# Output products of mixing and attention: seven products after Strassen in place of eight blocks, low parts of the right sums by accumulating DMA

## The chip, the cores and the metric

The kernel runs on one core of one Trainium2 chip. The metric is the time of one execution in microseconds of the device. The kernel before has a median of 1040.52 us over 3 runs (1040.29 to 1040.53).

## The reference

One decoder layer on 512 tokens of width 1024, in float32, each step followed by a layer norm of `alpha*h + sublayer(h)`:

1. a SwiGLU FFN at half weight (inner width 2816);
2. token mixing: one input projection, whose columns go to a gated linear recurrence in four heads of 128 (q, forget gate, input, output gate) and to causal pooling in four groups; the 512 columns of the heads and the 512 of the pooling are put side by side and mapped by `w_mix_out` (1024 x 1024);
3. cross-attention of four heads of 256 into 256 memory tokens, mapped by `wo` (1024 x 1024);
4. a second SwiGLU FFN at half weight.

```python
merged = jnp.concatenate([o, p], axis=-1); return merged @ w_out        # mixing
o = jnp.einsum('bhsm,bmhd->bshd', p, v).reshape(b_, s_, D_MODEL); return o @ wo   # attention
```

## The kernel before, in words

**Float32 by three products.** TensorE multiplies in a reduced float32 (`F32R`). So every operand x is split into a high part, a cast of x on ScalarE, and a low part, x minus the high part on VectorE (`split`, lines 66 to 68); a product is high x high + high x low + low x high, three matmuls into one PSUM bank (`mm3`, line 55). A weight block is 128 x 1024 (512 KB): `wblock` (lines 71 to 82) loads it from HBM on SP's queue into a raw tile and splits it.

**Tiles.** `b8` is a ring of 13 tiles of 8 KB per partition, `raw` and `q` are rings of 7 tiles of 4 KB (raw blocks; high or low parts), PSUM has six banks `mm` and two `tr`. The program order is a priority: the framework orders each engine's queue ahead of time by what it takes to be ready, so a later operation can be drawn forward while an earlier one waits. The queues themselves run in order.

**The two FFNs** already use Strassen's method with seven products for both of their matrices. For the output matrix (`strassen_gemm`, lines 325 to 454) the right-hand sums t1 to t4 of the weights are formed in HBM: `Sums` (lines 266 to 313) lists copies of a block into scratch and accumulating DMAs into it, all on POOL's queue. `one_behind` (lines 317 to 323) issues the next listed action behind a weight block, after a tiny POOL operation that reads this block; `pace` says behind which share of the blocks. The second FFN's 48 actions begin behind the query weights of mixing at a pace of 2/3 (lines 677 to 679); what is left is issued by `step` (line 304) inside the second FFN.

**Mixing.** Projections for the forget gates and queries (lines 669 to 682); pooled groups, gates and the levels of the scan (lines 703 to 837); states, head outputs and their norm (lines 842 to 890), with the keys of the memory, `mem_key(0)` to `(2)`, between them. The transposed head outputs are gated and split into `mg[0]`, `mg[1]` (lines 893 to 905); the pooled part was split into `mg[2]`, `mg[3]` as it came (lines 743 to 749).

**The output product** `out_gemm` (lines 206 to 258) runs for mixing (line 907) and attention (line 1000). The four row tiles of 128 tokens have 8 k tiles and two halves of 512 columns: 2 x 4 x 8 x 3 = 192 matmuls of 128 x 128 by 128 x 512. The first half runs block by block over all row tiles. The second keeps its four weight blocks and runs row tile by row tile; after each come the add into h, the statistics, the layer norm (`ln_tile`, lines 167 to 182, whose power is POOL's) and the transposes with their splits (`transpose_h`, lines 184 to 203), while the next row tile is multiplied.

**Around it.** After mixing come the memory keys 3 to 7 and the memory values (lines 910 to 927), which don't need h. Attention's loop is lines 984 to 998: queries (`xq`), `scores`, `attend` (the transposes of P and their split), `values`, which splits each head's output into `oT`. Attention's output product loads the second FFN's first two weight blocks through `pre` (line 1002).

Of the kernel before, what the change touches and what calls it, by code (L numbers as in the profile page):

```python
# [16 lines left out]
P = 128  # L17
S = 512
# [16 lines left out]
def layer_kernel(ctx: ExitStack, tc: tile.TileContext, a, out):  # L35
# [170 lines left out]
    def out_gemm(wsrc, nkt, act, alpha, g, b, eps, name, final=False, order=None, stay=4, ys=None, pre=None):  # L206
        nb = nkt // 2
        order = list(range(nb)) if order is None else order
        tiles = None
        stats = [st.tile([P, 2, 6], F32, tag=f"stats{t}", name=f"stats{t}", bufs=1) for t in range(NT)]  # L210
        for hf in range(2):
            ps = [None] * NT
            head = nb - (2 if hf == 0 else stay)

            def part(t, i, w):
                if ps[t] is None:
                    ps[t] = mm_ps(f"{name}ps{hf}{t}")
                hi, lo = w
                for j in range(2):
                    ah, al = act(order[i] * 2 + j)  # L220
                    tsl = slice(t * P, (t + 1) * P)
                    wh, wl = hi[:, j * 512:(j + 1) * 512], lo[:, j * 512:(j + 1) * 512]
                    nc.tensor.matmul(ps[t], ah[:, tsl], wh, start=i == 0 and j == 0, stop=False)  # L223
                    nc.tensor.matmul(ps[t], ah[:, tsl], wl, start=False, stop=False)  # L224
                    nc.tensor.matmul(ps[t], al[:, tsl], wh, start=False, stop=i == nb - 1 and j == 1)  # L225

            for i in range(head):
                w = wblock(wsrc[hf, order[i]], f"{name}{hf}_{i}")
                for t in range(NT):
                    part(t, i, w)  # L230
            ws = [wblock(wsrc[hf, order[i]], f"{name}{hf}_{i}", stay=hf == 1 and i < head + 3) for i in range(head, nb)]
            if hf == 1:
                GB = ln_bcast(g, b)
                if pre is not None:
                    pre()
            for t in range(NT):
                for i, w in enumerate(ws):
                    part(t, head + i, w)
                sl = slice(hf * 512, hf * 512 + 512)
                nc.vector.scalar_tensor_tensor(  # L240
                    out=h[t][:, sl], in0=h[t][:, sl], scalar=float(alpha), in1=ps[t],
                    op0=ALU.mult, op1=ALU.add)
                nc.vector.bn_stats(stats[t][:, hf, :], h[t][:, sl])
                if hf == 1:
                    ln_tile(t, stats[t], GB, eps)
                    if final:
                        for q in range(2):
                            nc.sync.dma_start(out[t * P:(t + 1) * P, q * 512:(q + 1) * 512], h[t][:, q * 512:(q + 1) * 512])
                    else:
                        if t == 0:  # L250
                            tiles = [quarter(f"{name}T{q}") if ys is not None else b8([P, 2, 2, S], F32R, f"{name}T{q}")
                                     for q in range(4)]
                        transpose_h(t, tiles, ys)
        if final:
            return None
        if ys is not None:
            return tiles
        return [(tiles[k // 2][:, k % 2, 0, :], tiles[k // 2][:, k % 2, 1, :]) for k in range(KT)]

# [6 lines left out]
    class Sums:  # L266


        def __init__(self, wsrc, name, kb1, kb2):
            self.w, self.name, self.kb1, self.kb2, self.T = wsrc, name, kb1, kb2, {}  # L270
            self.copies = [(p, b) for some in (("t1", "t3", "t2"), ("t4",)) for b in range(len(kb1)) for p in some]
            self.adds = list(self.copies)

# [51 lines left out]
    def strassen_gemm(groups, S_, alpha, g, b, eps, name, final=False, pre=None, ys=None):  # L325
# [61 lines left out]
        if len(groups) == 1:  # L387
            quarter_["s1"] = [raw4([P, 4, 256], f"{name}s1")]
        else:
            s1 = b8([P, 2, 4, 256], F32, f"{name}s1")  # L390
            s1_ = [sm.tile([P, n, 256], F32, tag="s1", name=f"{name}s1_{n}", bufs=2) for n in (2, 1)]
            quarter_["s1"] = [s1[:, 0], s1[:, 1], *s1_]
# [61 lines left out]
        return [(tiles[k // 2][:, k % 2, 0, :], tiles[k // 2][:, k % 2, 1, :]) for k in range(KT)]  # L454

# [212 lines left out]
    T0 = b8([P, H * S], F32, "T0")  # L668
    pf01 = proj_T2(wf, X1, "pf")
# [7 lines left out]
    sums2 = Sums(a["w2out"], "f2", *FFN_BLOCKS)  # L677
    todo_behind += sums2.actions()
    pace[:] = 0, 2, 3
# [35 lines left out]
    mg = {q: b8([P, 2, 2, S], F32R, f"mg{q}") for q in (2, 3)}  # L715

    def mslot(k):
        return mg[k // 2][:, k % 2, 0, :], mg[k // 2][:, k % 2, 1, :]

# [23 lines left out]
    def pool_out(g):  # L743
        pm = mm_ps("pm")
        nc.tensor.matmul(pm, pw[:, g, :], pooled[g], start=True, stop=True)
        mh, ml = mslot(4 + g)
# [119 lines left out]
    for q in range(2):  # L866
        mg[q] = b8([P, 2, 2, S], F32R, f"mg{q}")
# [211 lines left out]
```

## Time and profile before

| | us |
|---|---|
| median of 3 runs | 1040.52 |
| the profiled execution, as timed | 1040.28 |
| its span, first to last instruction | 1038.5 |
| PE busy | 1024.5 (99%), 6898 matmuls |
| DVE busy | 830.7 (80%), 1360 instructions |
| ACT busy | 508.3 (49%) |
| POOL busy | 137.4 (13%) |

Engines: PE is TensorE's matmuls, PEld its weight loads, DVE VectorE, ACT ScalarE, POOL GpSimd; SP's queue only issues DMAs. PE's busy time is modelled with overlapping ends: a matmul of 512 columns is shown with 0.39 us, and the next starts long before that. So its speed is read from start to start, and its waits from the list of waits. A window row gives, for a stretch, busy time and (number of instructions) of each engine, then the granted TensorE clock (1.00 is 2.4 GHz), the DMA engines' busy share and their GB/s. Mixing's output product lies at about 490 to 538 us, attention's at 644 to 694 us, the second FFN from 694 us on.

### The profile page before, as it was taken

How to read it: one execution, taken by the hardware profiler on the slowest of the kernel's cores; microseconds unless marked ns; L12 is line 12 of the kernel's file. 1: busy time of each engine (PE TensorE's matmuls, PEld its weight loads, DVE VectorE, ACT ScalarE, POOL GpSimd, SP SyncE). 2: the span in 40 equal slices, each digit the busy share in tenths (PEclk: the TensorE clock that was granted, in tenths of full speed). 3: DMA queues.
4: the chain of work that ended last, by engine and by line, in shares of the span. 5: the costliest groups of instructions: out<-in, count | busy, mean ns of one | idle time of the engine just before them, and what ended most of it. 6: DMA issues, size and time to landing. Idle time of an engine off the chain costs nothing. (4 is left out here: it accounts for less than half of the span.)

```text
span 1038.5 us, 17839 instructions
## 1 busy us (share of the span) xinstructions
PE 1024.5 (99%) x6898; PEld 926.9 (89%) x6898; DVE 830.7 (80%) x1360; ACT 508.3 (49%) x879; POOL 137.4 (13%) x212
## 2 busy tenths in 40 slices
PE   9999999999999999999999999999999999999995
PEld 8999999998887988879888988889999999988884
DVE  7999888889989645886686356589988888889885
ACT  5566555566644422235324345236555555565731
POOL 0011111215200101002212100110000000025000
PEclk9999999999999999999999999999999999999998
DMA  9375776578966455544819741603333332359761
GB/s 359 130 243 164 220 230 201 144 232 263 285 212 241 145 155 150 148 128 131 239 60 339 207 110 61 203 23 123 90 104 124 100 102 86 119 178 241 240 236 68
DMA packets 46148, 177.36 MB, mean 171 GB/s; under 512 B 6512, under 2 KB 7792, under 8 KB 42736
## 3 DMA queue, kind: packets, MB, share of 16 engines
q1 hardware_dynamic: 40176, 130.09, 36.3%
q0 software_dynamic: 5888, 46.14, 18.0%
q8 instruction: 54, 0.88, 0.3%
q14 instruction: 30, 0.25, 0.1%
HBM read 174.11 MB, written 48.23 MB: 214 GB/s over the span
## 5 line engine op out<-in xcount | busy, mean ns | idle before, releaser
L547 PE MATMUL f2u<-xt,qf2s 128*128 128x256 f32 x480 | 60.7, 283 | 0.0
L547 PE MATMUL f1u<-xt,qf1s 128*128 128x256 f32 x480 | 60.7, 283 | 0.0
L547 PEld LDWEIGHTS f1u<-xt,qf1s 128*128 128x128 f32 x480 | 59.0, 192 | 0.0
L547 PEld LDWEIGHTS f2u<-xt,qf2s 128*128 128x128 f32 x480 | 59.0, 192 | 0.0
L174 POOL TENSOR_TENSOR rstd<-ve,mhalf 128x1 f32<-128x1 f32 x16 | 15.6, 973 | 153.9 <-DVE ve L172 153.9
L68 DVE TENSOR_TENSOR wlo_wv<-raw_wv,whi_wv 128x1024 fp32r<-128x1024 f32 x12 | 14.7, 1224 | 23.4 <-PE pq L57 8.5
L547 PE MATMUL f2w<-xoT,qf2a 128*128 128x256 f32 x240 | 32.1, 284 | 0.0
L547 PE MATMUL f1u<-xT,qf1a 128*128 128x256 f32 x240 | 32.1, 283 | 0.0
L547 PE MATMUL f2u<-xoT,qf2a 128*128 128x256 f32 x240 | 32.1, 283 | 0.0
L547 PE MATMUL f1w<-xT,qf1a 128*128 128x256 f32 x240 | 32.1, 284 | 0.0
L307 POOL TENSOR_TENSOR seen<-qf2a,mhalf 128x1 f32<-128x1 f32 x10 | 5.9, 593 | 188.2 <-ACT qf2a L67 188.2
L547 PE MATMUL f1u<-xt,qf1a 128*128 128x256 f32 x240 | 30.7, 284 | 0.0
L547 PE MATMUL f1v<-xt,qf1s 128*128 128x256 f32 x240 | 30.7, 284 | 0.0
L547 PE MATMUL f2v<-xt,qf2s 128*128 128x256 f32 x240 | 30.4, 284 | 0.0
L547 PE MATMUL f1v<-xT,qf1s 128*128 128x256 f32 x240 | 30.4, 283 | 0.0
L547 PE MATMUL f2v<-xoT,qf2s 128*128 128x256 f32 x240 | 30.4, 284 | 0.0
L547 PE MATMUL f2u<-xt,qf2a 128*128 128x256 f32 x240 | 30.4, 283 | 0.0
L547 PEld LDWEIGHTS f1w<-xT,qf1a 128*128 128x128 f32 x240 | 30.3, 192 | 0.1
L547 PEld LDWEIGHTS f2w<-xoT,qf2a 128*128 128x128 f32 x240 | 30.3, 192 | 0.0
L547 PEld LDWEIGHTS f1u<-xT,qf1a 128*128 128x128 f32 x240 | 30.2, 192 | 0.0
L547 PEld LDWEIGHTS f2u<-xoT,qf2a 128*128 128x128 f32 x240 | 30.2, 192 | 0.0
L547 PEld LDWEIGHTS f1u<-xt,qf1a 128*128 128x128 f32 x240 | 29.6, 192 | 0.1
(435 smaller groups left out, 3305.8 us busy)
## 6 DMA issues: line engine op xcount, KB each, us to landing
f1t<-in_w1out POOLq DMA_DIRECT2D x30, 512.0 KB, 8.0
f2t<-in_w2out POOLq DMA_DIRECT2D x30, 512.0 KB, 6.6
raw_f1t<-f1t SPq DMA_DIRECT2D x20, 512.0 KB, 4.4
raw_f2t<-f2t SPq DMA_DIRECT2D x20, 512.0 KB, 4.9
raw_f2g<-in_w2in SPq DMA_DIRECT2D x17, 512.0 KB, 3.7
raw_f2u<-in_w2in SPq DMA_DIRECT2D x17, 512.0 KB, 3.8
raw_f1u<-in_w1in SPq DMA_DIRECT2D x15, 512.0 KB, 5.9
raw_f1b<-in_w1out SPq DMA_DIRECT2D x15, 512.0 KB, 7.5
```

Source lines behind the costliest of these rows:

```text
L68: nc.vector.tensor_tensor(out=lo, in0=src, in1=hi.bitcast(F32), op=ALU.subtract)
L174: nc.gpsimd.tensor_tensor(out=rstd, in0=ve, in1=mhalf[:, 0:1], op=ALU.pow)
L307: ins = nc.gpsimd.tensor_tensor(out=seen, in0=q[:, 0, 0:1].bitcast(F32), in1=mhalf[:, 0:1], op=ALU.mult).ins
L547: nc.tensor.matmul(o, q[:, w, wsl], x[k][r], start=opens and k == 0 and n == 0, stop=ends and k == 3 and n == 2, skip_group_check=True)
```

## The change

Both calls of `out_gemm` become `strassen_heads`, and `out_gemm` goes. With A cut into token halves and k halves, and the weights into k halves and column halves, the seven products are a11 x b11, s1 x t1, s2 x t2, a12 x b21, s4 x b22, s3 x t3 and a22 x t4; s1 to s4 are formed on VectorE in place. They go into six PSUM banks (u, v, w, two row tiles each); u and v are added into h in between, and u is opened a second time for a22 x t4. For this, the pooled part, the head outputs and the attention outputs are kept as plain float32 (`mgp`, `mgh`, `OT`) and no longer split when they come.

The t blocks of both matrices are formed in HBM by `Sums`, as the FFNs' are: 16 actions for each matrix, listed ahead of the second FFN's 48. Their split is different (`by_dma`): ScalarE writes the high part, and then minus the high part into the low part's tile; a DMA on POOL's queue adds the raw block from HBM onto that. These blocks stay in `b8` tiles until used. t1 and t2 of mixing are split after `mem_key(0)` and before `mem_key(1)`, those of attention after the last queries; t3 and t4 inside the product. The memory keys 3 to 7 are handed to mixing's product as `fill`, ahead of its transposes.

```diff
-    def wblock(src, name, stay=False):
+    def wblock(src, name, stay=False, by_dma=False):
...
-        split(raw, hi, lo)
+        if by_dma:
+
+            nc.scalar.copy(out=hi, in_=raw)
+            nc.scalar.activation(lo, hi.bitcast(F32), AF.Copy, scale=-1.0)
+            nc.gpsimd.dma_start(lo, src, accum_op=ALU.add, max_dma_last_dim=8192)
+        else:
+            split(raw, hi, lo)
...
+    def sum_blocks(S_, name, *which):
+
+        for p in which:
+            for i in range(2):
+                assert (p, i) in S_.T and (p, i) not in S_.adds
+                S_.ready[p, i] = wblock(S_.T[p, i], f"{name}{p}{i}", True, True)
+
+    def strassen_heads(A1, A2, S_, alpha, g, b, eps, name, ys=None, fill=None, pre=None):
...
+        product(left("a11"), "b11", u, True)
+        combine("s1", "a21", "a22", ALU.subtract)
+        L = left("s1")
+        for t in range(2):
+            add(t, 0, u[t], True)
+        product(L, "t1", v, True)
+        combine("a21", "a11", "a21", ALU.subtract)
+        combine("a11", "s1", "a11", ALU.subtract)
+        L = left("a11")
+        for t in range(2):
+            add(2 + t, 1, v[t], True)
+        product(L, "t2", u)
+        L = left("a12")
+        for t in range(2):
+            add(t, 1, u[t], True, ALU.subtract)
+        product(L, "b21", w, True, True)
+        combine("a12", "a12", "a11", ALU.add)
+        L, L3 = left("a12"), left("a21")
+        for t in range(2):
+            add(t, 0, w[t], False, last=True)
+        B22 = list(right("b22"))
+        sum_blocks(S_, name, "t3", "t4")
+        L4, T3, T4 = left("a22"), list(right("t3")), list(right("t4"))
+        GB = ln_bcast(g, b)
+        for t in by_tiles(L, B22, v, True):
+            add(t, 1, v[t], False, last=True)
+            ln_tile(t, stats[t], GB, eps)
+        for t in by_tiles(L3, T3, u):
+            add(2 + t, 1, u[t], False, ALU.subtract, last=True)
+        tiles = [quarter(f"{name}T{q}") if ys is not None else b8([P, 2, 2, S], F32R, f"{name}T{q}") for q in range(4)]
+        if fill is None:
+            transpose_h(0, tiles, ys)
+        for t in by_tiles(L4, T4, u, True):
+            if fill is None and t == 0:
+                transpose_h(1, tiles, ys)
+            add(2 + t, 0, u[t], True, last=True)
+            ln_tile(2 + t, stats[2 + t], GB, eps)
+            if t == 0 and pre is not None:
+                pre()
+        if fill is not None:
+            fill()
+        for t in range(0 if fill is not None else 2, NT):
+            transpose_h(t, tiles, ys)
...
+    sums_mo = Sums(a["wmixo"], "mo", [2, 3], [0, 1])
+    sums_xo = Sums(a["wo"], "xo", [0, 1], [2, 3])
+    sums2 = Sums(a["w2out"], "f2", *FFN_BLOCKS)
+    todo_behind += sums_mo.actions() + sums_xo.actions() + sums2.actions()
+    pace[:] = 0, 1, 1
     pf01 = proj_T2(wf, X1, "pf")
...
-    sums2 = Sums(a["w2out"], "f2", *FFN_BLOCKS)
-    todo_behind += sums2.actions()
-    pace[:] = 0, 2, 3
...
     mem_key(0)
+    pace[:] = 0, 0, 1
+    sum_blocks(sums_mo, "mo", "t1")
...
+    sum_blocks(sums_mo, "mo", "t2")
     for k in range(1, 3):
         mem_key(k)
...
+    def more_keys():
+        pace[:] = 0, 4, 5
+        for k in range(3, KT):
+            mem_key(k)
+
+    pace[:] = 0, 0, 1
+    X2 = strassen_heads(mg[1], mg[0], sums_mo, ALPHA, a["ln2_g"], a["ln2_b"], LN_EPS, "mo", fill=more_keys)
...
     xq(3)
+    pace[:] = 0, 0, 1
+    sum_blocks(sums_xo, "xo", "t1", "t2")
...
+    X3 = strassen_heads(*OT, sums_xo, ALPHA, a["ln3_g"], a["ln3_b"], LN_EPS, "xo", ys=ys,
+                        pre=lambda: wx.extend(wblock(a["w2in"][u * FT], f"f2{'gu'[u]}0") for u in range(2)))
```

In the functions that are not shown, `left(p)` splits a quarter of A into a `b8` tile, `right(p)` gives the two blocks of b11, b21, b22 by `wblock` or the ready blocks of a sum, `product` runs block by block over both row tiles, `by_tiles` row tile by row tile, and `add` adds a bank into h and, at the last add of a half, takes its statistics.

## Rows read from the trace of the kernel before

**Rows 1.** The page, from its head and its first part: the span, and busy time (share of the span) and instructions of an engine.

```profile
span 1038.5 us, 17839 instructions
...
PE 1024.5 (99%) x6898; PEld 926.9 (89%) x6898; DVE 830.7 (80%) x1360; ACT 508.3 (49%) x879; POOL 137.4 (13%) x212
```

**Rows 2.** The timeline of PE in mixing's query projections, the first and the last of 96 matmuls of 512 columns: start (us), shown duration (us), engine, line, operation, out<-in, shapes, count.

```profile
361.29 0.39 PE L56 MATMUL pq<-f1T,whi_wq 128*128 128x512 f32 x1
...
382.83 0.39 PE L58 MATMUL pq<-f1T,wlo_wq 128*128 128x512 f32 x1
```

**Rows 3.** The list of waits of PE between 340 and 720 us, all of it: tile and line that waited <- engine, tile and line that released it: us in total, times, longest.

```profile
PE trh L192 <- DVE h L180: 0.5, 1, 0.5
PE po L56 <- ACT PT L67: 0.2, 1, 0.2
```

**Rows 4.** Windows of 20 us: PE, PEld, DVE, ACT, POOL busy (instructions), granted clock, DMA share, GB/s.

```profile
540.00:560.00 20.00, 20.00 (x144) 18.72 (x143) 15.49 (x26) 9.68 (x17) 4.97 (x9) 1.00 0.86 277
560.00:580.00 20.00, 20.00 (x107) 17.28 (x106) 10.44 (x11) 9.16 (x11) 4.30 (x10) 1.00 1.01 334
...
660.00:680.00 20.00, 19.50 (x90) 15.91 (x89) 13.30 (x20) 2.32 (x3) 1.00 (x2) 1.00 0.34 122
680.00:700.00 20.00, 20.00 (x122) 17.29 (x121) 17.82 (x32) 7.58 (x13) 2.96 (x3) 1.00 0.08 27
700.00:720.00 20.00, 19.97 (x166) 19.57 (x165) 17.92 (x29) 11.88 (x21) 0.00 (x0) 1.00 0.38 133
```

**Rows 5.** Windows again, with the instructions alone that touch the output product's banks: mixing's, then attention's. The first pair is PE's matmuls, then PEld and DVE.

```profile
480.00:550.00 70.00, 45.72 (x192) 35.63 (x192) 5.48 (x8) 1.00 0.50 148
...
640.00:700.00 60.00, 45.47 (x192) 35.84 (x192) 5.48 (x8) 1.00 0.30 97
```

**Rows 6.** Groups of DVE between 480 and 700 us, by line: out<-in, shapes, count | busy us, mean ns of one | idle us before them and who ended it.

```profile
L177 DVE SCALAR_TENSOR_TENSOR h<-h,mv,G 128x512 f32<-128x512 f32 x16 | 11.2, 744 | 0.0
L243 DVE BATCH_NORM_STATS2 stats<-h 128x6 f32<-128x512 f32 x16 | 11.1, 693 | 0.4
L180 DVE SCALAR_TENSOR_TENSOR h<-h,rstd,B 128x512 f32<-128x512 f32 x15 | 10.6, 746 | 0.1
...
L240 DVE SCALAR_TENSOR_TENSOR h<-h,xops 128x512 f32<-128x512 f32 x8 | 5.5, 684 | 4.3 <-PE xops L225 4.3
...
L68 DVE TENSOR_TENSOR wlo_mo<-raw_mo,whi_mo 128x1024 fp32r<-128x1024 f32 x4 | 4.9, 1219 | 1.1 <-issue 1.1
L68 DVE TENSOR_TENSOR xoT<-trh,xoT 128x512 fp32r<-128x512 f32 x6 | 4.1, 688 | 2.3 <-ACT xoT L67 2.3
...
L900 DVE SCALAR_TENSOR_TENSOR og<-ot,gn,GS 128x512 f32<-128x512 f32 x4 | 2.9, 745 | 0.0
...
L170 DVE BATCH_NORM_AGGREGATE mv<-stats 128x2 f32<-128x12 f32 x8 | 1.6, 205 | 0.1
...
L172 DVE TENSOR_SCALAR ve<-mv 128x1 f32<-128x1 f32 x8 | 1.2, 153 | 0.2
```

**Rows 7.** The timeline of ACT: two casts of 1024 columns in mixing's product, the two casts of P after the queries, the copy of a head's output.

```profile
494.89 1.99 ACT L67 CAST ws_mo<-raw_mo 128x1024 fp32r<-128x1024 f32 x2
...
630.04 1.07 ACT L67 CAST PT<-pt 128x512 fp32r<-128x512 f32 x2
...
646.47 0.59 ACT L67 CAST oT<-po 128x512 fp32r<-128x512 f32 x1 [2.16 <-PE po L58]
```

**Rows 8.** The timeline of PE around the end of the head outputs and of the attention outputs: the first output matmul drawn in, the last transposes; the first output matmul drawn in, the last of the values.

```profile
490.38 0.48 PE L223 MATMUL mops<-whi_mo,mg 128*128 128x512 f32 x1
...
492.91 0.60 PE L898 MATMUL ot<-ident,o 128*128 128x128 f32 x4
...
644.44 0.40 PE L223 MATMUL xops<-whi_xo,oT 128*128 128x512 f32 x1
...
647.18 0.39 PE L58 MATMUL po<-PT,VM 128*128 128x512 f32 x1
```

**Rows 9.** The list of waits of ACT in the second FFN, from 740 to 900 us, a line of it.

```profile
ACT qf2s L67 <- PE f2u L547: 19.6, 31, 0.8
```

**Rows 10.** The timeline of POOL: the issue of a sum in HBM, beside mixing's product.

```profile
491.74 0.85 POOL L290 DMA_DIRECT2D f2t<-f2t  x1 [0.30 <-issue]
```

**Rows 11.** DMA: a queue's packets, MB, share of 16 engines; then issues, out<-in, queue, count, KB each, median us from issue to landing.

```profile
q0 software_dynamic: 5888, 46.14, 18.0%
...
f1t<-in_w1out POOLq DMA_DIRECT2D x30, 512.0 KB, 8.0
...
raw_f2u<-in_w2in SPq DMA_DIRECT2D x17, 512.0 KB, 3.8
...
raw_f1u<-in_w1in SPq DMA_DIRECT2D x15, 512.0 KB, 5.9
...
f2t<-f2t POOLq DMA_DIRECT2D x10, 512.0 KB, 7.3
...
raw_mo<-in_wmixo SPq DMA_DIRECT2D x8, 512.0 KB, 3.8
```

**Rows 12.** Windows of the first and of the second FFN, amid their inner products; columns as in rows 4.

```profile
140.00:160.00 20.00, 20.00 (x169) 20.00 (x168) 17.27 (x33) 11.38 (x22) 3.19 (x5) 1.00 0.70 212
780.00:800.00 20.00, 20.00 (x169) 20.00 (x168) 17.27 (x33) 11.39 (x22) 0.63 (x1) 1.00 0.26 79
```

More of the change, by code (lines that the diff above doesn't have):

```diff
@@ L203, in transpose_h @@
                 nc.scalar.copy(out=ys[t // 2][:, t % 2, hf * 4:hf * 4 + 4, :], in_=ps.rearrange("p (k n) -> p k n", k=4))
[L206 to L258, printed above, removed]
@@ L272, in __init__ @@
             self.adds = list(self.copies)
+            self.ready = {}
         def copy(self, behind):
@@ L386, in strassen_gemm @@
         L = left("a11")
[L387 to L392, printed above, removed]
+        s1 = b8([P, 2, 4, 256], F32, f"{name}s1")
+        s1_ = [sm.tile([P, n, 256], F32, tag="s1", name=f"{name}s1_{n}", bufs=2) for n in (2, 1)]
+        quarter_["s1"] = [s1[:, 0], s1[:, 1], *s1_]
         product(L, "b11", u, True)
@@ L712, in layer_kernel @@
         nc.vector.tensor_tensor(out=QP[:, hd, :], in0=QP[:, hd, :], in1=T0[:, hd * S:(hd + 1) * S], op=ALU.mult)
-    mg = {q: b8([P, 2, 2, S], F32R, f"mg{q}") for q in (2, 3)}
-    def mslot(k):
-        return mg[k // 2][:, k % 2, 0, :], mg[k // 2][:, k % 2, 1, :]
+    mg = [None, b8([P, 4, S], F32, "mgp")]
     pooled = {}
@@ L745, in pool_out @@
         nc.tensor.matmul(pm, pw[:, g, :], pooled[g], start=True, stop=True)
[L746 to L749 removed]
+        nc.scalar.activation(mg[1][:, g, :], pm, AF.Copy, scale=psc[:, g:g + 1])
     pool_in(3)
@@ L864, in layer_kernel @@
         states.append(Sn)
-    for q in range(2):
-        mg[q] = b8([P, 2, 2, S], F32R, f"mg{q}")
+    mg[0] = b8([P, 4, S], F32, "mgh")
     os_ = []
@@ L898, in layer_kernel @@
             nc.tensor.transpose(pt[:, hs], o[:, hs], ident)
-        og = sm.tile([P, S], F32, tag="sg", name="og")
         nc.vector.scalar_tensor_tensor(
-            out=og.rearrange("p (h d) -> p h d", h=H), in0=pt.rearrange("p (h d) -> p h d", h=H),
+            out=mg[0][:, :, cs], in0=pt.rearrange("p (h d) -> p h d", h=H),
             scalar=gn[:, 0:1], in1=GS[:, :, cs], op0=ALU.mult, op1=ALU.mult)
-        ov = og.rearrange("p (a b n) -> p a b n", a=2, b=2)
-        for q in range(2):
-            split(ov[:, q], mg[q][:, :, 0, cs], mg[q][:, :, 1, cs])
-    X2 = out_gemm(a["wmixo"], KT, mslot, ALPHA, a["ln2_g"], a["ln2_b"], LN_EPS, "mo", order=[2, 3, 0, 1])
-    for k in range(3, KT):
-        mem_key(k)
+    def more_keys():
[4 more added lines that the diff above has]
+    X2 = strassen_heads(mg[1], mg[0], sums_mo, ALPHA, a["ln2_g"], a["ln2_b"], LN_EPS, "mo", fill=more_keys)
     VM = [b8([P, 2, D], F32R, f"VM{q}") for q in range(2)]
@@ L980, in values @@
                 mm3(po, VM[m][:, 0, csl], VM[m][:, 1, csl], PT[:, m, 0, :], PT[:, m, 1, :], m == 0, m == 1)
-            split(po, oT[:, j, 0, :], oT[:, j, 1, :])
-        OT[hd] = oT
+            nc.scalar.copy(out=OT[hd // 2][:, 2 * (hd % 2) + j, :], in_=po)
     xq(0)
@@ L999, in layer_kernel @@
     ys, wx = [], []
-    X3 = out_gemm(a["wo"], KT, lambda k: (OT[k // 2][:, k % 2, 0, :], OT[k // 2][:, k % 2, 1, :]),
-                  ALPHA, a["ln3_g"], a["ln3_b"], LN_EPS, "xo", ys=ys,
-                  pre=lambda: wx.extend(wblock(a["w2in"][u * FT], f"f2{'gu'[u]}0") for u in range(2)))
+    pace[:] = 0, 0, 1
+    X3 = strassen_heads(*OT, sums_xo, ALPHA, a["ln3_g"], a["ln3_b"], LN_EPS, "xo", ys=ys,
+                        pre=lambda: wx.extend(wblock(a["w2in"][u * FT], f"f2{'gu'[u]}0") for u in range(2)))
     todo_behind.clear()
```

54 lines of the change are left out of this document (49 added, 5 removed).

## The prediction

> **What bounds the kernel now.** I read the page first: TensorE (PE) is busy 1024.5 of 1038.5 us, and VectorE (DVE) 830.7 [rows 1]. Busy PE time is modelled, so I went to the timeline for the start times. In one projection the first and the last of 96 matmuls of 512 columns start 21.54 us apart, which is 0.227 us from start to start, and nothing stands between them [rows 2]. The list of PE's waits between 340 and 720 us has two entries, 0.7 us together [rows 3]. So here PE is the bound almost everywhere: a matmul taken away is a gain, and any new wait of PE is a loss. The windows by stage say what is close behind. Between 540 and 720 us DVE has 10 to 18 of 20 us, most of it (17.8 and 17.9) from 680 us on, where attention's output product ends and the second FFN begins; the DMA engines are at 0.86 to 1.01 between 540 and 580 us, and the granted clock is full [rows 4].
>
> **What the change removes.** Each of the two output products has 192 matmuls of 512 columns [rows 5]. Seven products of half size, each 2 row tiles x 4 k tiles x 3 matmuls = 24, are 168. That is 24 less per product, 48 in all: 48 x 0.227 = 10.9 us of PE. Nothing else of PE's work changes. With no new wait the profiled execution's own 1040.28 us would become 1029.4. It stands 0.24 us below the median of the runs shown, 1040.52; I add that at the end.
>
> **What it adds on DVE.** Prices: 1.2 us for 1024 columns, 0.69 for an add into h or a statistic, and for one layer norm 0.2 + 0.15 + 2 x 0.74 + 2 x 0.75 = 3.3 [rows 6]. From the start of product t1 to the end of t4 PE has six products, 6 x 24 x 0.227 = 32.7 us. In the same stretch DVE has 3 combinations and 5 splits of 1024 columns (9.6 us), the low parts of b21 and b22 (4 blocks, 4.8), 12 adds (8.3), 6 statistics (4.1) and two layer norms (6.7): 33.5 us. The low parts of the eight t blocks are no longer DVE's; they would have been 9.6 us more. DVE and PE are thus even in this stretch, and each hand-over that is not covered shows on PE. There are four places.
>
> (a) *The first left sum.* Before t1, the chain from the last data is: in mixing og 0.75, combination 1.2, cast on ScalarE (ACT) 1.05 [rows 7], subtraction 1.2, and some 0.1 for each of four hand-overs, 4.6 us. PE covers it with a11 x b11, 24 matmuls. In the kernel before, 8 output matmuls were already drawn in among the four transposes; then 16 x 0.227 = 3.6 us are left, and PE waits 1.0. In attention a copy (0.59) takes the place of og: 4.4 us, against 21 matmuls or 4.8 us left, since three were drawn ahead there [rows 8]. I take 1.0 + 0. Bounds: 0, if other work is drawn in; 4.6 + 4.4 = 9.0, if all of b11 has run before.
>
> (b) *t4 writes into the banks that t3 filled.* Those must first be added into h. In program order these adds stand behind both layer norms of the first two row tiles, which begin when the first half of b22 is done. From there DVE has 2 x (0.69 + 0.69 + 3.3) + 0.69 = 10.1 us; PE has half of b22 and t3, 8.2 us. In attention that is 1.9 us of waiting, and I take 2.0. In mixing the memory keys can run in the freed banks of w; I take 0.5. Bounds: 0, if DVE takes the adds as soon as they are ready; 3.3 each, if one more layer norm goes first.
>
> (c) *The tail of attention.* The second FFN's first projection needs its weights' low parts (2 x 1.2), and these now stand behind the splits of two row tiles' transposes (4 x 0.69) and one add, statistic and layer norm (4.7): 9.9 us of DVE, against t4 and 16 transposes on PE, 5.4 + 2 = 7.4. I take 2.4. Before, PE had a full 24 matmuls for each row tile here. Bounds: 0 and 5 (a second layer norm in front). What is late next is the second FFN's quadrants, which can bear it: their splits wait for buffers that PE frees, 19.6 us in 160 [rows 9]. In mixing's tail the memory keys (5 x 24 matmuls) and the values stand behind the product and cover the layer norms: nothing, and about 3 us if their weights' splits come late.
>
> (d) *t1 and t2 on ACT beside the scan and the queries.* Each block costs ACT two passes of about 1.05 us, 16.8 us for these eight, where the softmax and the casts of P stand too [rows 7]. POOL's accumulating DMA, some 0.8 us to issue [rows 10], waits for the second pass; behind it in POOL's queue stand the powers for the norms, and DVE and then PE wait for those. I take 0.5 for each stage, because single ACT operations are delayed and PE has keys and queries to fill with. Bounds: 0, and 4.2 for each (four passes in front of one cast that PE needs).
>
> **Costed at nothing.** The copies and sums in HBM grow from 48 to 80, and of the second FFN's 48, which mostly ran up to 660 us before, all but a few move into that FFN. Each takes about 2.1 us of all 16 engines (18.0% of 1038.5 us for 46.14 MB) [rows 11]. The first FFN already runs its own in this way: its DMA share is 0.70 against 0.26, and PE is busy 20.00 of 20 us in both [rows 12]. Its weight loads take 5.9 instead of 3.8 us [rows 11], which the run-ahead of [rows 9] hides. Between 540 and 580 us the pace rises from 2/3 to 4/5, some three more actions, or 6 us of a full DMA; loads ahead of use cover this, otherwise it costs up to those 6 us. SP issues 12 more weight loads (28 for 16); a load of a t block waits on its sum, with the next weights queued behind it, but all of mixing's sums are issued by the 16th weight block, long before. POOL issues 16 more DMAs and 32 more copies and sums, beside which nothing but the norms' powers waits on it. DVE loses the splits of og, of po and of the pooled part, eight of 256 and twelve of 512 columns, some 12 us at the prices above; that is spare time in those stages, so I count no gain.
>
> The sum: 1040.28 - 10.9 + 1.0 (a) + 2.5 (b) + 2.4 (c) + 1.0 (d) = 1036.3, and 0.24 more as a median: **1036.5 us**.
>
> **The accumulating DMA** from HBM into SBUF does not occur in this trace. The nearest rows are the plain 512 KB load, 3.8 us, and the sum in HBM, 7.3 us [rows 11]. I take the second, which also reads its destination. The slots for t3 and t4 come free at the latest when t2 ends; b21 and b22 follow, 10.9 us. Two ACT passes (2.1) and the issue (0.8) take 2.9 of them, so up to 8.0 us from issue to landing costs nothing. The Trainium skill (DMA: Bandwidth & Descriptors, Anatomy of one DMA) gives such a DMA about 2 us plus its bytes at 436 GB/s, by estimate 3.2 us for 512 KB. These rows show twice that for accumulating ones, so the measurement decides; by the page the margin would be larger and the sum the same.
>
> **The rivals.** *All hidden* (0.18): the engines' queues are ordered ahead of time by what is ready, as the matmuls drawn in at (a) show. If that also moves the adds of (b) and the weights of (c) forward, only (a) is left: 1030.6. Against it: DVE has no spare time from t1 to t4.
> *DVE takes the gain* (0.22): (b) at 3.3 twice and (c) at 5, which is 12.6 with (a): 1042.2 at the far end, 1038.5 to 1042.5. For it: 17.8 of 20 us already at 680 [rows 4].
> *The low parts come late* (0.13, slower): the mechanism lies at t3. Over 8.0 us of landing PE waits for the excess in each product; beyond 8.0 + 3.1 = 11.1 us the two waits eat the remaining 4.0 and 2.1 more, and the kernel is slower. At 14.6, twice the sum in HBM, the waits are 2 x 6.6 and the time 1049.7. Against it: the medians of POOL's DMAs are at most 8.0 [rows 11], and the DMA engines are lightly used from 660 to 700 us [rows 4]. The change would then also not do what it says, since the work would only be moved from DVE into a wait.
> *The clock* (0.05, slower): all windows of the kernel before show the full level, but it has no wait of PE over 0.5 us there [rows 3]. If a wait at (a), (b) or (c) lets the clock fall to the lower of its two levels, 1.2 instead of 2.4 GHz, each product run there costs another 5.4 us; two, with the stalls, give 1047. The Trainium skill (TensorE: Matmul & The Clock Gate, The HAM clock gate) says that an idle PE goes back to half clock; no row here shows it within the work.
>
> **How the numbers follow.** The forecast's case (0.42) is 1033.5 to 1038.4. The range 1031 to 1043 holds it, the DVE case and most of the hidden one, and leaves out the late DMA and the clock (0.18) and a little below. About 2.1 us (0.2%) is what a measurement can tell from no change. Faster takes the forecast and the hidden case, 0.60; the same is the DVE case, 0.22; slower the last two, 0.18. The likeliest case's own range is 1033.5 to 1038.4.
>
> **What would show it.** PE has 48 matmuls fewer at an unchanged 0.227 us. Its waits name DVE: the split of the left sum before t1, the add into h before t4, the low part of f2g before the projection. If they name the accumulating DMA or POOL instead, the third rival holds; if DVE's are absent and the time is near 1030, the first. The second FFN's DMA share should rise from about 0.3 to 0.7 without PE losing anything; a wait of PE there, or a granted clock below full, would make the prediction wrong.

## The result, and the profile after

The changed kernel takes 1044.99 us (median of five, 1044.25 to 1046.64) against 1040.52 for the kernel before: a ratio of 1.0044, interval 1.0032 to 1.0056. It is slower by 0.4%, where I forecast 1036.5 and at most 1043. The profiled execution is the one of 1044.99 us.

The head and the first part of the page after, beside [rows 1]: PE has the 48 matmuls fewer that were counted, ACT 35 us more, DVE 10 us more.

```profile
span 1043.2 us, 17910 instructions
...
PE 1019.9 (98%) x6850; PEld 922.2 (88%) x6850; DVE 840.8 (81%) x1370; ACT 543.4 (52%) x913; POOL 169.1 (16%) x260
```

PE's waits after, 340 to 720 us. Where [rows 3] has two entries, 0.7 us together, there are now eight, 11 waits of 14.1 us:

```profile
PE mou L442 <- DMA ws_mot<-mot: 4.4, 2, 2.2
PE xou L442 <- DMA ws_xot<-xot: 2.5, 2, 1.5
PE pk L58 <- DVE wlo_wk L68: 2.4, 1, 2.4
PE ot L953 <- DVE mgh L954: 2.3, 1, 2.3
PE pk L56 <- ACT whi_wk L67: 1.0, 1, 1.0
PE po L56 <- ACT PT L67: 0.6, 1, 0.6
PE pt L1024 <- DVE e L1016: 0.5, 2, 0.3
PE f2p L56 <- ACT xoT L67: 0.4, 1, 0.4
```

The waits are not all. Windows after, columns as in [rows 4]; the last two cover what follows the waits at 491 and at 547 us:

```profile
480.00:500.00 20.00, 17.61 (x121) 15.59 (x120) 14.45 (x28) 12.91 (x44) 5.85 (x6) 0.91 0.82 208
520.00:540.00 20.00, 15.63 (x75) 12.36 (x74) 15.53 (x26) 5.15 (x6) 5.57 (x8) 1.00 1.00 261
540.00:560.00 20.00, 16.67 (x111) 16.00 (x110) 15.05 (x27) 7.61 (x13) 8.25 (x9) 0.83 0.67 212
680.00:700.00 20.00, 17.47 (x80) 13.88 (x79) 16.85 (x29) 6.76 (x10) 3.68 (x4) 1.00 0.83 210
780.00:800.00 20.00, 20.00 (x169) 20.00 (x169) 18.19 (x36) 11.06 (x22) 3.34 (x5) 1.00 0.63 184
...
494.60:498.00 3.40, 3.31 (x10) 2.20 (x9) 3.33 (x5) 0.16 (x1) 0.00 (x0) 0.50 0.48 100
549.30:556.00 6.70, 5.87 (x27) 5.87 (x28) 5.12 (x7) 1.79 (x5) 3.84 (x2) 0.50 0.98 373
```

Twice the granted clock is at its lower level, 3.4 and 6.8 us long, right behind waits of PE. To add up waits and clock I took, from PE's timeline, every matmul's start minus the start before it, less its pitch at full clock (0.227 us for 512 columns, 0.12 for 256, 0.11 for 128), and summed what is left by stretch of each kernel:

| us lost by PE | before | after | more | the prediction's step |
|---|---|---|---|---|
| 480 to 500 | 0.5 | 4.9 | 4.4 | (d), 0.5, (a) and the clock |
| 520 to 540 | 1.0 | 5.1 | 4.1 | low parts late, 0 |
| 540 to 560 | 0.5 | 6.4 | 6.0 | mixing's tail, 0 |
| 640 to 660 | 0.6 | 2.9 | 2.3 | (d), 0.5 |
| 680 to 700 | 0.7 | 3.2 | 2.4 | low parts late, 0 |
| 700 to 720 | 0.6 | 2.0 | 1.4 | (c), 2.4 |
| the whole kernel | 21.6 | 40.8 | 19.1 | |

The stretches that are not listed win 1.5 us back. So 10.9 us are gained and 19.1 lost. PE's last matmul starts at 1026.46 us before and at 1035.00 after, 8.5 us later. The time rose by only 4.5, because the two kernels end differently. These records stand in the two traces after PE's last matmul (start, duration, engine; not counted as busy, so no row of the page has them):

```
before  1028.78  8.94  GpSimd DRAIN        after  1037.32  2.99  GpSimd DRAIN
before  1033.61  0.01  Sync   DRAIN        after  1042.46  0.01  Sync   DRAIN
```

The kernel ends when both are through. In the kernel before SP had its outputs out at 1033.61, but POOL's drain lasted until 1037.72. After, POOL is done at 1040.31 and SP, which has the outputs, ends last.

Where the losses come from can be read in five places. ACT at the scan, beside [rows 7]: four passes for t1 stand ahead of the first state's copy (`krT`). The first line is the kernel before, the others the changed one.

```profile
474.57 0.59 ACT L850 COPY krT<-krt 128x512 f32<-128x512 f32 x1
...
473.91 2.00 ACT L82 CAST ws_mot<-raw_mot 128x1024 fp32r<-128x1024 f32 x2
475.81 2.00 ACT L83 ACTIVATE ws_mot<-ws_mot 128x1024 fp32r<-128x1024 f32 x2
477.71 0.57 ACT L905 COPY krT<-krt 128x512 f32<-128x512 f32 x1
```

PE at the scan's end, beside [rows 8], and ACT's cast of the pooled part (`moa`). Before, seven output matmuls ran between 490.38 us and the next transposes at 492.21, while DVE gated the first head outputs. Now none does: the pooled part is no longer split as it comes, but here:

```profile
490.01 1.03 PE L953 MATMUL ot<-ident,o 128*128 128x128 f32 x8
493.34 0.63 PE L953 MATMUL ot<-ident,o 128*128 128x128 f32 x4 [2.29 <-DVE mgh L954]
493.72 0.48 PE L442 MATMUL mou<-whi_mob,moa 128*128 128x512 f32 x1
...
490.48 1.05 ACT L67 CAST moa<-mgp 128x1024 fp32r<-128x1024 f32 x1
```

ACT and POOL ahead of mixing's t3. The last matmul of t2 starts at 512.2 us and the first of t3 at 523.32; both high parts of t3 are cast before the first is negated, and the two accumulating DMAs follow 0.94 us apart:

```profile
513.59 1.99 ACT L82 CAST ws_mot<-raw_mot 128x1024 fp32r<-128x1024 f32 x2
515.49 2.00 ACT L83 ACTIVATE ws_mot<-ws_mot 128x1024 fp32r<-128x1024 f32 x2
...
516.84 1.80 POOL L84 DMA_DIRECT2D ws_mot<-mot  x2 [25.36 <-DVE wlo_mob L68]
```

They landed at 525.83 and 529.69 us, 9.0 and 11.9 us after their issue, and PE's two waits end at 525.87 and 529.73.

DVE in mixing's tail: the low part of a key's weights behind a whole layer norm. PE ran the first two keys ahead of it and stopped at the third.

```profile
547.53 1.41 DVE L186 SCALAR_TENSOR_TENSOR h<-h,rstd,B 128x512 f32<-128x512 f32 x2
548.86 1.22 DVE L68 TENSOR_TENSOR wlo_wk<-raw_wk,whi_wk 128x1024 fp32r<-128x1024 f32 x1
```

DMA issues, beside [rows 11] (the last figure is the median from issue to landing): a plain load of a sum's block, the accumulating DMA onto it in SBUF, the sum in HBM.

```profile
q0 software_dynamic: 9984, 71.31, 28.5%
...
raw_f2g<-in_w2in SPq DMA_DIRECT2D x17, 512.0 KB, 5.4
...
raw_mot<-mot SPq DMA_DIRECT2D x8, 512.0 KB, 4.8
ws_mot<-mot POOLq DMA_DIRECT2D x8, 512.0 KB, 9.9
...
ws_xot<-xot POOLq DMA_DIRECT2D x8, 512.0 KB, 11.3
mot<-mot POOLq DMA_DIRECT2D x4, 512.0 KB, 7.4
```

### The profile page after: what moved, and what is told of

It reads as the page before. It is cut to its first block, busy times and chain, and to the rows that moved or that the text cites. A ratio compares the mean times of both kernels' runs of the same rounds, so it can differ in the third digit from the quotient of the medians.

```text
span 1043.2 us, 17910 instructions
## 1 busy us (share of the span) xinstructions
PE 1019.9 (98%) x6850; PEld 922.2 (88%) x6850; DVE 840.8 (81%) x1370; ACT 543.4 (52%) x913; POOL 169.1 (16%) x260
## 4 chain that ended last, share of the span: by engine, by line
PE 89%; issue 4%; DMA 3%; DVE 2%; ACT 2%; POOL 1%; DVEq 0%; POOLq 0%; ACTq 0%
PE f1u L605 11%; PE f2u L605 11%; PE f1u L320 6%; PE f2u L320 6%; PE f1v L605 6%; PE f2v L605 6%; PE f1v L320 3%; PE f2v L320 3%; PE f2w L605 3%; PE f1w L605 3%; PE mou L442 1%; PE f1w L320 1%; PE f2w L320 1%; DMA ws_xot<-xot 1%; PE pxq L56 1%
## 5 line engine op out<-in xcount | busy, mean ns | idle before, releaser
L260 POOL TENSOR_TENSOR seen<-qf1a,mhalf 128x1 f32<-128x1 f32 x10 | 5.6, 556 | 180.7 <-ACT qf1a L67 137.7
```

The lines of the kernel that those rows point to most:

```text
L260: ins = nc.gpsimd.tensor_tensor(out=seen, in0=q[:, 0, 0:1].bitcast(F32), in1=mhalf[:, 0:1], op=ALU.mult).ins
```

## The experiments

My theory: four separate losses, (1) ACT's two passes per sum block ahead of the scan and the values, (2) t3's low parts landing late, (3) the key weights' low parts behind the layer norms on DVE, (4) the clock behind the waits of (1) and (3). Rivals: DVE is the bound inside the products; or attention loses it.

All runs together, each beside the kernel before on its chip (medians 1040.5 to 1040.8). The last four columns are of the profiled execution: its time, PE's last matmul, DMAs on POOL's queue, POOL's last DRAIN. The profiled execution need not be near the median: e2, e3 and e11 are 2.3 to 3.5 us above it, e16 3.2 below.

| kernel | us (median) | ratio, interval | profiled | PE's last matmul | DMAs | DRAIN |
|---|---|---|---|---|---|---|
| e1 mixing alone | 1052.17 | 1.0093 to 1.0123 | 1051.37 | 1035.56 | 120 | 10.91 |
| e2 attention alone | 1041.50 | 1.0001 to 1.0020 | 1043.84 | 1028.06 | 120 | 10.91 |
| e3 all split by ACT and DVE | 1044.66 | 1.0025 to 1.0060 | 1047.11 | 1030.68 | 128 | 11.56 |
| e4 no accumulating DMA for t3, t4 | 1036.65 | 0.9947 to 0.9975 | 1036.59 | 1026.61 | 136 | 2.33 |
| e5 t3 earlier | 1034.96 | 0.9927 to 0.9960 | 1034.97 | 1024.97 | 144 | 2.99 |
| e6 keys earlier | 1039.40 | 0.9980 to 0.9999 | 1039.23 | 1029.20 | 144 | 2.99 |
| e7 before, 34 DMAs more | 1035.47 | 0.9937 to 0.9966 | 1035.00 | 1025.31 | 130 | 1.85 |
| e8 second pass on POOL | 1060.15 | 1.0172 to 1.0202 | 1059.84 | 1049.83 | 144 | 2.99 |
| e9 t3, keys | 1039.38 | 0.9979 to 0.9998 | 1040.08 | 1030.08 | 144 | 2.99 |
| e10 t3, keys, t1 | 1037.18 | 0.9957 to 0.9982 | 1036.26 | 1026.27 | 144 | 2.99 |
| e11 t3, keys, t1, t2 | 1036.41 | 0.9953 to 0.9976 | 1039.87 | 1029.87 | 144 | 2.99 |
| e12 t3, t1 | 1032.10 | 0.9900 to 0.9930 | 1032.87 | 1022.87 | 144 | 2.99 |
| e13 t3, t1, three keys | 1034.61 | 0.9915 to 0.9948 | 1036.23 | 1026.22 | 144 | 2.99 |
| e15 t3, t1, t2 | 1032.98 | 0.9906 to 0.9935 | 1032.82 | 1022.82 | 144 | 2.99 |
| e16 e3, 2 DMAs more | 1039.98 | 0.9977 to 1.0000 | 1036.76 | 1026.78 | 130 | 1.85 |
| e17 before, 30 DMAs more | 1042.76 | 1.0010 to 1.0031 | 1042.76 | 1026.49 | 126 | 11.40 |

**Which part loses (e1, e2).** Each takes one call of `strassen_heads` back to `out_gemm`.

```diff
-    X3 = strassen_heads(*OT, sums_xo, ...)      # cut short; e1;  e2: X2 in the same way
+    X3 = out_gemm(a["wo"], KT, ...)
```

> Mixing's output product by seven products as in the changed kernel, attention's as before. My theory: mixing loses more than its 24 matmuls give. From the gaps between PE's matmuls in the changed kernel (beyond the kernel before): 4.4 us at 480-500 (the wait at the scan's end, then half clock), 4.1 at t3, 6.0 in the tail, 14.5 in all against 24 x 0.227 = 5.4 gained, so PE's last matmul comes 9 us later than in the kernel before; the kernel's end was 4 us earlier against PE's last matmul in the changed kernel (POOL's last drain), so 1045.5 to 1049.5 us. Rival (each part loses its own half, since both have the same late low parts): 1042 to 1043.5. Rival (attention loses it): below 1040.

> Attention's output product by seven products as in the changed kernel, mixing's as before. My theory: the gaps give 2.0 us at 640-660 (ACT's passes for t1 and t2), 2.9 at t3 and 1.4 at FFN2's start, 6.3 against 5.4 gained: PE's last matmul 0.9 us later than in the kernel before, and 1037.5 to 1041.5 us with or without the 4 us that POOL's last drain held. Rival (each part loses its own half): 1042 to 1043.5.

By PE's last matmul the theory holds: 9.1 us later than before with mixing alone, 1.6 with attention alone. As e2's profiled execution is 2.3 us above its median, attention by itself about breaks even for PE. The times are higher than expected by the drain, 10.91 us in both, which ends 6.0 us behind SP's outputs. So e1 came out above its range, mixing alone being 11.4 us slower though the whole change is only 4.5, and e2 at the upper end of its own.

**Low parts by DVE (e3), and no accumulating DMA for t3 and t4 (e4).** e4 leaves these DMAs out, so its products t3 and t4 are not the right ones; it only gives the time.

```diff
-                S_.ready[p, i] = wblock(S_.T[p, i], f"{name}{p}{i}", True, True)
+                S_.ready[p, i] = wblock(S_.T[p, i], f"{name}{p}{i}", True)          # e3
...
-            nc.gpsimd.dma_start(lo, src, accum_op=ALU.add, max_dma_last_dim=8192)
+            if 't1' in name or 't2' in name:                                        # e4
+                nc.gpsimd.dma_start(lo, src, accum_op=ALU.add, max_dma_last_dim=8192)
```

> All eight sums' low parts by ACT's copy and DVE's subtraction, as the other weights have it, no accumulating DMA into SBUF. My theory: the waits at t3 (4.1 and 2.9 us) go, half of ACT's passes ahead of the scan go (2 of 4, about 2 us of the 4.4), and DVE takes 16 x 1.22 = 19.5 us more, of which what is ahead of t3 (4 x 1.22 = 4.9 us in each part) comes back as a wait of 0 to 3 us in each: 1037 to 1044 us, likeliest 1041. Rival (DVE is the bound inside the products, the reason that the low parts were given to the DMA): 1047 or more.

> The accumulating DMAs of t3 and t4 left out in both parts (their low parts stay minus the high part, so the products t3 and t4 are not computed rightly); all else as in the changed kernel. It prices the late landing alone. My theory: 4.1 us in mixing and 2.9 in attention come back, 7 in all: 1038 us. Rival (another chain, DVE's splits of the left sums, is as late there): 1043 or more.

e4 gains 8.3 us, somewhat more than expected: nothing else was late at t3, and the late landing is priced, with what follows from it (the stretch at the lower clock in mixing's tail is 3.4 us long in its trace, not 6.8). In e3 the waits of PE between 340 and 720 us begin so:

```profile
PE ot L953 <- DVE mgh L954: 2.4, 1, 2.4
PE mou L442 <- DVE h L462: 1.8, 1, 1.8
PE pk L56 <- ACT whi_wk L67: 1.4, 1, 1.4
PE xou L442 <- DVE h L462: 1.3, 1, 1.3
```

The DMA is gone from the list, and the adds into h before t4, step (b) of the prediction, appear in its place. PE's last matmul comes 4.3 us earlier than in the changed kernel, but its drain of 11.56 us hides that. So the rival is true in part: DVE with these low parts costs 3.1 us at t4, less than the late DMA. One part of the theory failed: half of ACT's passes ahead of the scan are gone, yet the wait at the scan's end is 2.4 us, no shorter than in the changed kernel, and DVE has these low parts between the states now (476 to 486 us).

**t3 earlier (e5), keys earlier (e6).**

```diff
             add(2 + t, 1, v[t], True)
+        sum_blocks(S_, name, "t3")                     # e5
         product(L, "t2", u)
...
-        sum_blocks(S_, name, "t3", "t4")
+        sum_blocks(S_, name, "t4")
...
+        for k in range(3, 5):                          # e6, ahead of t4's product
+            wks[k] = wblock(a["wk"][k], f"wk{k}")
```

> The changed kernel with the split of t3 moved two products ahead (behind the split of the second left sum, ahead of the product with t2), in both parts; t4 stays. My theory (the low parts of t3 land too late, because ACT's eight passes for t3 and t4 and the DMA's 10 us stand in the one product before them): the waits at t3 (4.7 us in mixing, 2.9 in attention) go and t4's with them, 1036.5 to 1038.5 us. Rival (ACT's passes, now ahead of the left sums' casts, make products wait instead): 1041 or more.

> The changed kernel with the weights of memory keys 3 and 4 loaded and split ahead of t4's product and the last two layer norms of mixing, instead of behind them. My theory: the two waits of PE in mixing's tail (1.1 and 2.6 us) go, and with them the stretch of half clock behind them (6.8 us long, some 2.5 to 3.4 of loss): 1038.5 to 1041.5 us. Rival (DVE is full there, so the layer norms come later by what the keys take, and PE waits for them at the transposes or at u): 1043.5 or more.

e6 holds, with 5.6 us. e5 gains 10.0, more than its range: besides the 6.9 us of waits for the DMA, the stretch at the lower clock in mixing's tail shrinks from 6.8 to 3.4 us. In e5 no wait for the accumulating DMA is left:

```profile
PE ot L954 <- DVE mgh L955: 2.3, 1, 2.3
PE pk L56 <- ACT whi_wk L67: 1.7, 1, 1.7
PE f2p L56 <- ACT xoT L67: 1.3, 1, 1.3
```

In e6 the window of 540 to 560 us has the full clock (it was 0.83), so the tail's waits and its half clock went together.

**The second pass on POOL (e8).**

```diff
-            nc.scalar.activation(lo, hi.bitcast(F32), AF.Copy, scale=-1.0)
+            nc.gpsimd.tensor_scalar(lo, hi.bitcast(F32), -1.0, None, op0=ALU.mult)
```

> The changed kernel with the second of the two passes for each sum block (minus the high part) on POOL instead of ACT. My theory: ACT's four passes ahead of the scan become two, so the scan's end comes 2 us earlier, attention's values 1, and the low parts at t3 land up to 4 us earlier (POOL works beside ACT), which halves the waits there: 1038 to 1041 us if a pass takes POOL 2 us or less. Rival (POOL takes 4 us or more for one, or slows DVE, and the DMA behind it starts later): 1045 or more.

The time is the rival's, though a pass of 3.2 us, where ACT takes 1.0, lies between the two conditions. PE waits 12.8 us for the accumulating DMAs instead of 6.9, and 4.8 instead of 2.3 at the scan's end, and the clock is at its lower level for 20.5 us instead of 10.2. The group of POOL (busy us, mean ns; idle before):

```profile
L83 POOL TENSOR_SCALAR ws_mot<-ws_mot 128x1024 fp32r<-128x1024 f32 x8 | 24.6, 3158 | 53.2 <-ACT ws_mot L82 53.2
```

**POOL's last drain (e7, e17, e16).** e7 and e17 are the kernel before with 34 and 30 more DMAs, e16 is e3 with two more:

```diff
+    more = scr.tile([34, D], F32, name="more")
+    for i in range(34):
+        nc.gpsimd.dma_start(more[i:i + 1, :], h[3][0:1, :])
     todo_behind.clear()
```

> The kernel before with 34 more DMAs of 4 KB each on POOL's queue ahead of the second FFN (130 instead of 96), nothing else. In six traces the last DRAIN of POOL takes 8.94 us with 96 DMAs on POOL's queue, 10.91 with 120 (twice), 11.56 with 128, but 2.33 with 136 and 2.99 with 144: 0.082 us for each, and starting over after 128. If it is the count that sets it: a drain of 1.8 to 1.9 us here, which then ends ahead of the output's DMAs, and the kernel ends 4 us earlier, 1036 to 1037 us, with PE's work unchanged. Rival (it goes by descriptors or bytes, of which these have nearly none): 1040.5 or slightly more.

> The kernel before with 30 more DMAs of 4 KB on POOL's queue (126), four fewer than the run with 130 that took 1035.47 us. My theory: a drain of 11.4 us (0.082 for each of 30 more than the 8.94 of 96), 2.5 us later end than the kernel before: 1042.5 to 1043.5 us. Rival (more DMAs shorten the drain by something other than their count): 1035.5 to 1040.

> The kernel with all eight sums' blocks split by ACT and DVE (1044.66 us, 128 DMAs on POOL's queue, a last DRAIN of 11.56 us) with two more DMAs of 4 KB on POOL's queue ahead of the second FFN: 130. My theory (the drain goes by the count of POOL's DMAs and starts over after 128): a drain of 1.85 us, no longer the last to end, and 1037.5 to 1039 us from two more DMAs. Rival (the drain goes by the bytes or by where the last DMA lies): 1044 to 1045.

The count sets the drain. From 126 to 130 DMAs it falls from 11.40 to 1.85 us, and the same kernel goes from 1042.76 to 1035.47. That is 0.5 us below e7's range, as PE's last matmul came 1.2 us earlier too, which stays open. e16's drain fell as expected, from 11.56, but the time by 4.7 us, to 1039.98, 1 us above the range: its ten executions go from 1036.31 to 1041.15, with mean granted clocks of 0.998 down to 0.993. The two traces of this split show where such a spread can come from. e3's (1047.11 us) has three stretches of 3.4 us at the lower clock, behind the waits at the scan's end (2.4 us), at t4 (1.8) and at the keys (1.4 and 0.8); e16's (1036.76 us) has the same waits, equally long, and the full clock. Windows of e3 and of e16:

```profile
520.00:540.00 20.00, 18.16 (x80) 14.94 (x79) 18.34 (x31) 2.11 (x2) 2.81 (x4) 0.91 0.44 146
...
520.00:540.00 20.00, 17.37 (x92) 14.65 (x90) 19.90 (x35) 2.17 (x4) 3.82 (x5) 1.00 0.43 136
```

So one and the same wait costs the clock in one execution and not in another; what decides it stays open.

**The moves together (e9, e10, e11).** e10 adds to e9 (t3 and two keys) the move of mixing's t1, e11 to e10 that of t2:

```diff
         if li == 5:
             memory()
+            pace[:] = 0, 0, 1
+            sum_blocks(sums_mo, "mo", "t1")            # e10, taken from behind mem_key(0)
...
         product(left("a11"), "b11", u, True)
+        if ("t2", 0) not in S_.ready:
+            sum_blocks(S_, name, "t2")                 # e11, taken from ahead of mem_key(1)
```

> Both moves on the changed kernel: t3's split two products ahead (1034.96 us alone) and the weights of keys 3 and 4 split ahead of t4's product. My theory: with t3 early the tail of mixing still shows a wait of 1.8 us at the keys and 0.91 of the full clock in 540 to 560 (1.8 us lost), and this goes: 1031 to 1032 us. Rival (the two moves take the same time from DVE or the DMA engines, and t3's gain is partly lost): 1034 to 1036.

> The kernel with both moves, and mixing's t1 split ahead of the scan's last levels (behind the loads of the memory) instead of behind them, so that ACT makes its four passes between the gates, where it is idle, and not ahead of the first state's copy. My theory: the first state's copy comes 3 us earlier, and PE's wait at the scan's end (2.4 us, with 0.91 of the full clock in 480 to 500 behind it, 1.8 us) shrinks or goes: 2 to 4 us less than the kernel with the two moves, 1027.5 to 1030. Rival (the scan's end is held by t2's four passes between the squares, which stay): no more than 1 us less.

> As the kernel with t3, the keys and t1 moved, and mixing's t2 split behind the first left sum's cast, after the scan, so that ACT has none of the sums' passes in the scan. My theory: the squares end 2 to 4 us earlier, the rest of the wait at the scan's end goes, 1026.5 to 1029 us. Rival (t2's low parts, now cast some 8 us later, land behind their product's start, 11 us after the first, and ACT's passes delay the second left sum): a wait at t2 of 2 to 6 us, as slow as the kernel with the two moves or slower.

e9 is a miss for the theory: 4.4 us slower than e5 alone. On top of it t1's move gains 2.2 us; t2's gives 0.8, less than e11's own executions differ by (1035.91 to 1039.87). Since both build on e9, both stay far above their ranges. In e9's timeline of DVE both layer norms now stand ahead of the third key's low part, and PE waits 3.5 us for it; in e5 two low parts came before the last norm. First e9, then e5:

```profile
541.57 1.41 DVE L186 SCALAR_TENSOR_TENSOR h<-h,rstd,B 128x512 f32<-128x512 f32 x2
...
544.68 1.40 DVE L186 SCALAR_TENSOR_TENSOR h<-h,rstd,B 128x512 f32<-128x512 f32 x2
546.00 1.22 DVE L68 TENSOR_TENSOR wlo_wk<-raw_wk,whi_wk 128x1024 fp32r<-128x1024 f32 x1
```

```profile
542.24 1.18 DVE L68 TENSOR_TENSOR wlo_wk<-raw_wk,whi_wk 128x1024 fp32r<-128x1024 f32 x1
...
544.71 1.22 DVE L68 TENSOR_TENSOR wlo_wk<-raw_wk,whi_wk 128x1024 fp32r<-128x1024 f32 x1
...
546.39 0.75 DVE L186 SCALAR_TENSOR_TENSOR h<-h,rstd,B 128x512 f32<-128x512 f32 x1 [0.46 <-POOL rstd L180]
```

**The order of the tail (e12, e13, e15).** e12 is e10 without the move of the keys, e13 is e10 with three keys, e15 is e12 with t2 moved as in e11.

> The changed kernel with t3's split two products ahead and mixing's t1 split ahead of the scan's last levels; the keys' weights stay where the change put them. In the kernel with t3 alone moved, DVE's queue in mixing's tail has two of the keys' low parts ahead of the last layer norm; with the keys moved too they all came behind both, and PE waited 3.6 us there. My theory (the tail's loss hangs on this order of DVE's queue): here the order is that of the kernel with t3 alone, and t1's gain of 2 to 4 us adds to it, 1031 to 1033 us. Rival (the gains of the moves don't add, whatever the order, since DVE is full through the tail): 1036 to 1037.5, as with all three.

> All three moves, with three keys' weights (3 to 5) ahead of t4's product in place of two. My theory: the third key's product, which waited 3.6 us for its low part behind both layer norms, no longer does; the fourth's low part comes behind them as the third's did, but PE is busy with the third key's product (24 matmuls of 256 columns, 2.9 us) by then, so 1 us or less of the wait is left, and the half clock behind it goes: 1032 to 1034.5 us. Rival (DVE's 1.22 us for the third low part puts off the layer norms, and the transposes wait): 1036 or more.

> As the kernel with t3 and t1 moved, and mixing's t2 split after the scan, behind the first left sum's cast. My theory: what ACT's passes for t2 take from the scan (1.1 us of PE's wait at the scan's end with t1 moved) goes, and t4 lands 1 us later: within 1 us of the kernel with t3 and t1 moved. Rival (it is the squares of the scan that hold its end): 1 us or more less than that.

e12 is the fastest of all, 8.5 us below the kernel before. It has the same work as e10, which took 5.1 us more, so the order of DVE's queue decided, not its load. Its ACT has the first state's copy at 474.95 us, and the wait at the scan's end is 1.0 with the full clock behind it:

```profile
PE pk L56 <- ACT whi_wk L67: 1.7, 1, 1.7
PE ot L954 <- DVE mgh L955: 1.0, 1, 1.0
PE f2p L56 <- ACT xoT L67: 0.7, 1, 0.7
...
PE mou L442 <- DVE moa L68: 0.6, 1, 0.6
```

```profile
480.00:500.00 20.00, 18.44 (x131) 16.73 (x130) 15.33 (x29) 9.21 (x39) 5.00 (x5) 1.00 0.56 133
```

What waits are left there are not DVE's lateness: it gates the first head outputs no later than in the kernel before. First the kernel before, then e12:

```profile
491.32 1.40 DVE L900 SCALAR_TENSOR_TENSOR og<-ot,gn,GS 128x512 f32<-128x512 f32 x2
...
490.96 1.40 DVE L955 SCALAR_TENSOR_TENSOR mgh<-ot,gn,GS 128x512 f32<-128x512 f32 x2
```

The 1.7 us at the keys are what is left in the tail, with 3.4 us at the lower clock behind them in this trace; e15's has the same wait and the full clock. e13 moved the wait on to the fourth key, at 2.4 us, not the 1 us or less that I expected. e15 equals e12 within 1 us, so t2's passes don't hold the scan's end.

## Why the prediction was wrong

I had PE gain 10.9 us and lose 6.9; it lost 19.1. So its last matmul came 8.5 us later instead of 4.0 earlier, and the end of the kernel gave 4.1 us of that back. The steps that failed are three that stood at nothing or close to it: the low parts at t3, mixing's tail, and (d).

- *The removal* was right: 48 matmuls.
- *(a) and (b)* cost nothing where I had put them: no wait of the changed kernel names the first left sum or the adds before t4. But (a) took it that output matmuls would again be drawn in among mixing's transposes. Two are, against eight before, as the pooled part is split only behind the scan, and PE waits at the transposes instead (see (d)). The mechanism of (b) is real once DVE has the low parts: 1.8 and 1.3 us in e3, against 0.5 and 2.0.
- *(c)*: attention's tail cost 1.4 for 2.4, and the wait there (0.4 us; 1.3 in e5) names the split of the transposes, not the low part of f2g. For mixing's tail I named the keys as the cover of the layer norms and 3 us if their splits came late. They did, and it cost 6.0, as the clock fell behind the wait; e6 got 5.6 back. The step that failed is taking as cover a stage whose own weights stood in the queue that it was to cover.
- *(d)* is the largest miss of a priced term: 1.0 for both stages, and the two stretches lost 4.4 + 2.3 = 6.7. My upper bound, 4.2 for each, described what happened (four passes in front of one cast that PE needs); I chose near zero because PE could fill in other work. ACT's passes are not all of it, though. With t1's moved away the first stretch loses 2.3 us instead of 4.9 (e12; e10 and e13 the same), and 2.2 without t2's as well (e15), against 0.5 before. So 2.6 of the 4.4 are t1's passes and the lower clock behind the wait. The rest, 1.8, is there even though DVE gates as early as before, and I put it down to the cover that is missing under (a); no run puts the early split back, so this part is read from the traces and not shown by a run. For attention e3, with one ACT pass for a block instead of two, bears (d) out: the stretch loses 1.2 us instead of 2.9.
- *The accumulating DMA*: I took 7.3 us and called up to 8.0 free. The price was that of sums issued one by one; the two of mixing's t3, 0.94 us apart, took 9.0 and 11.9. And they left late: I had two ACT passes between the end of t2 and the issue, 2.1 us, but ACT first made two casts of left operands and both casts of t3, and the issue came 4.4 us after t2 (512.44 to 516.84). The first wait, 2.2 us, is nearly all this delay, the second the longer landing. I put all of it in the rival alone, at 0.13; its formula on the medians (9.9 and 11.3) gives waits of 1.9 and 3.3, and measured were 4.4 and 2.5 (in attention one at t3 and one at t4). The estimate of 3.2 us by the Trainium skill (DMA: Bandwidth & Descriptors, Anatomy of one DMA) was further off than the row; the plain load took 4.8.
- *The clock*: it fell behind the 2.3 us wait at 491 us and again in mixing's tail. That agrees with the Trainium skill (TensorE: Matmul & The Clock Gate, The HAM clock gate), that an idle PE goes back to half clock; but after the two waits of 2.2 us at 523 and 527 us the window of 520 to 540 us has the full clock, and e3 and e16 differ with equal waits. I had it as a rival of 0.05 by itself; it is rather a surcharge on (c) and (d), 10.2 us at half speed in all and so at most 5.1 us, by estimate.
- *Costed at nothing* held in the second FFN: a DMA share of 0.63 and PE busy 20.00 of 20 us at 780 to 800 us, raw_f2g at 5.4 us.
- *Not seen at all*: the end of the kernel before was POOL's drain, not PE's work. Against e7, where the drain is out of the way, the change costs 1044.99 - 1035.47 = 9.5 us (8.5 by PE's last matmul); and the best version, e12, gains 3.4 of its 8.5 us by its work (3.6 by PE's last matmul) and the rest by the drain.

The rivals "low parts come late" and "the clock" both happened, each smaller than I had priced it alone, and together with (d) and mixing's tail they made the sum negative. I had added chances where the losses add.

## What to carry to other kernels

When a method trades matmuls for preparation, price each preparing pass in the queue where it will stand, and look for the one chain (here a scan) that has no cover there; a bound that describes the actual order is the estimate. When an operand is kept whole to be split later, ask which matmuls its early split had fed. Late data was mended by issuing it two products earlier, for 10 us, but this and the move of the keys did not add: together they changed the order of DVE's queue, and t3's and t1's moves alone were faster. Look also at what ends last after the last matmul, before and after: an engine's drain can be worth as much as the change.

## What the runs showed of the hardware

POOL's last DRAIN grows by 0.082 us for each DMA on POOL's queue and drops between 128 and 130: 8.94 us with 96, 10.91 with 120 (twice), 11.40 with 126, 11.56 with 128, 1.85 with 130 (twice), 2.33 with 136, 2.99 with 144. It is the count, as the DMAs added in e7, e16 and e17 had 4 KB each.

A pass over 128 x 1024 elements took POOL 3.2 us (one input, e8), ACT 1.0 and DVE 1.2 (two inputs).

An accumulating DMA of 512 KB into SBUF landed after 5.3 to 5.5 us where it was issued more than 7 us from the next (e12, 467 to 487 us). Of two issued 0.95 us apart in the changed kernel, the first landed after 6.8 to 9.0 and the second took 2.8 to 3.9 us more; a further pair right behind took 11.7 to 14.5. The plain load of the same blocks took 4.8 and 7.2 there (medians).

Waits of PE of 1.8 to 2.4 us were followed by 3.4 us at half clock in e3 and by the full clock in e16, at the same places.
